# One gather of joined up and down rows per expert slot, with coefficients slot by slot on ScalarE

## The chip, the cores and the metric

The kernel runs on one core of a Trainium2 chip. The metric is the device time of one execution in microseconds (us). The engines are named as in the profile: PE (TensorE), PEld (its weight loads), DVE (VectorE), ACT (ScalarE), POOL (GpSimd) and SP (SyncE, which issues most DMAs). DMAs with indices computed on the chip are issued by POOL.

## What is computed

One layer of a streaming encoder on 512 tokens of width 2048: two groups of attention heads, then a mixer that picks experts by product keys. The change touches the expert part only. Per token, 8 heads pick 16 experts each out of 16384; an expert is one row of `u` and one row of `v`.

```python
def peer_sublayer(h, w_query, sub_keys, u, v):
    def block(hb):                                   # 128 tokens
        ...
        idx = jnp.take_along_axis(cand_i, best_j, axis=-1)        # 8 heads x 16 experts
        g = jax.nn.softmax(best_s, axis=-1)
        u_sel = jnp.take(u, idx, axis=0)
        a = jax.nn.gelu(jnp.einsum('thkd,td->thk', u_sel, hb), approximate=False)
        v_sel = jnp.take(v, idx, axis=0)
        return jnp.einsum('thk,thkd->td', (g * a).astype(hb.dtype), v_sel)
```

So per token and slot (a head's pick) there is an "up" step, the dot product of the token with a row of `u`, a Gelu and a gate, and a "down" step that adds the coefficient times a row of `v`.

## The kernel before

Attention and the projections take the first 1304 us; the change doesn't touch them. The experts are then computed in two ways side by side.

*Dense, on PE* (352 of the 512 tokens): all experts in 128 groups `j`. An **A** item multiplies the 352 tokens by the `u` of one group (48 matmuls of 352 columns, L1030), takes the Gelu on ACT and stores it to DRAM as `a_scr` (L902, L905). The last 16 products are **D** items, whose result stays on the chip. A **V** item multiplies gated activations by one half of a group's `v` (24 matmuls, L1044). Between V items, **R** items load a group's activations and gates and multiply them (`gated`: `gb` on DVE at L1049, hi part `ph` on ACT at L1051; `low`: `pl` on DVE at L1056). Every operand is split into a hi and a lo part (`split`: hi cast `wh` on ACT, L190; lo part `wl` on DVE, or for some V items on POOL, L191). Four buffers each hold a cut of weights `wh`, `wl`; an A item uses four cuts, a V item two. `cut_up` prepares the item after the one that PE works on. The gates reach the dense part by a scatter: DVE sums the gates of equal experts (`junk`, L950), and POOL writes them with 384 indirect DMAs of 128 single numbers each (L962). These are spread over the A items, four or five pieces an item. The scatters of one head wait for those of the head before.

*Sparse, by gathers* (the other 160 tokens): 160 **slots** of 128 partitions, 128 slots for the first 128 tokens ("f") and 32 for the other 32 tokens, spread over the partitions ("x"). For each slot a gather on POOL fetches 128 rows of `u` and another 128 rows of `v`, 8 KB a row, 1 MB a gather (L849). The up step is a multiply with a sum along the row on DVE (L869, followed by the read of its accumulator), the down step a multiply and add on DVE (L871). The steps go in blocks of 16: 16 up steps, then one Gelu on ACT and one multiply by the gates on DVE for all 16 slots (L874, L875), then 16 down steps. That makes 320 steps. `due` hands them out in proportion to the work of the items; a step is popped between two cuts of an A item, or after the cuts of a V item. The gather buffers are three of 8 KB a partition, and a gather is issued two steps ahead.

```python
    def consume(i):
        ...
        ahead(i + 2)
        ...
    gt = ctx.enter_context(pool("gt", 3))
```

The order on PE, DVE, ACT and SP is the order in which the code is written (`fixed`, L1081). On POOL a scheduler sets it.

Of the kernel before, what the change touches and what calls it, by code (L numbers as in the profile page):

```python
# [9 lines left out]
F32 = mybir.dt.float32  # L10
# [85 lines left out]
def hymba_peer(ctx: ExitStack, tc: tile.TileContext, xT, w_in, w_fl, b_fg, g_mix, g_q, g_k, g_merge,  # L96
               w_out, g_ffn, w_q, keysT, uT, u, v, out):
# [759 lines left out]
    def consume(i):
        if i == 0:
            ahead(0)
            ahead(1)  # L860
        ahead(i + 2)
        st, n = steps[i]
        x, s = order[st][n]
        if (st, n) == ("x", 0):
# [12 lines left out]
        yield  # L877

# [4 lines left out]
    steps = [("f", n) for n in range(2 * P)] + [("x", n) for n in range(2 * SL)]  # L883
# [3 lines left out]
    def due(n, hold=False):  # L887
# [4 lines left out]
        return [consume(i) for i in r]  # L892
# [46 lines left out]
    gt = ctx.enter_context(pool("gt", 3))  # L939
# [57 lines left out]
    def load(t):  # L997
        if t >= len(items):
# [4 lines left out]
            [(f"v{it[2]}", v[j * P:j * P + P, it[2] * H:it[2] * H + H])]  # L1003
# [143 lines left out]
def arrays_of(i):  # L1147
# [20 lines left out]
    a["u"] = c(uu.reshape(P, P, D).transpose(1, 0, 2).reshape(P * P, D))  # L1168
    a["v"] = c(np.asarray(i["peer_v"])[0].reshape(P, P, D).transpose(1, 0, 2).reshape(P * P, D))
# [20 lines left out]
```

## Time and profile before

| | us |
|---|---|
| median of 3 runs (3423.48 to 3425.88) | 3423.88 |
| the profiled execution | 3414.49 |
| its span, first to last instruction | 3412.8 |
| stretch with the scatters (1333 to 2162) | 829 |
| rest of the U products (2162 to 2394) | 232 |
| V products (2394 to the end) | 1019 |

| Engine | busy us | share |
|---|---|---|
| PE | 3259.3 | 96% |
| DVE | 2506.0 | 73% |
| POOL | 1566.5 | 46% |
| ACT | 1283.6 | 38% |

A share over the whole span is a mean over stretches with different limits, so it is read stretch by stretch. Busy time leaves out the issue of DMAs on SP and the gaps between instructions. "Idle before, releaser" is the time in which an engine stood still before an instruction, and what ended it; "issue" means that nothing in the trace ended it.

### The profile page before, as it was taken

How to read it: one execution, taken by the hardware profiler on the slowest of the kernel's cores; microseconds unless marked ns; L12 is line 12 of the kernel's file. 1: busy time of each engine (PE TensorE's matmuls, PEld its weight loads, DVE VectorE, ACT ScalarE, POOL GpSimd, SP SyncE). 2: the span in 40 equal slices, each digit the busy share in tenths (PEclk: the TensorE clock that was granted, in tenths of full speed). 3: DMA queues.
4: the chain of work that ended last, by engine and by line, in shares of the span. 5: the costliest groups of instructions: out<-in, count | busy, mean ns of one | idle time of the engine just before them, and what ended most of it. 6: DMA issues, size and time to landing. Idle time of an engine off the chain costs nothing.

```text
span 3412.8 us, 52962 instructions
## 1 busy us (share of the span) xinstructions
PE 3259.3 (96%) x19406; PEld 3057.5 (90%) x19406; DVE 2506.0 (73%) x4536; ACT 1283.6 (38%) x2452; POOL 1566.5 (46%) x1134
## 2 busy tenths in 40 slices
PE   8999999999999999988889888999999999999998
PEld 6888888888888899988888888899999999999998
DVE  7555656567547996766666666678899989899995
ACT  5544545443333333322222222334333333333332
POOL 2000000013226866787877887422444544544452
PEclk9999999999999999999999999999999999999999
DMA  3333223332443236888778777899999999998995
GB/s 121 125 102 108 91 97 104 107 103 87 144 136 112 93 127 229 293 271 275 264 263 272 268 260 269 289 339 338 375 384 363 367 368 376 353 366 348 380 362 177
DMA packets 233702, 810.85 MB, mean 238 GB/s; under 512 B 38080, under 2 KB 92480, under 8 KB 191936
## 3 DMA queue, kind: packets, MB, share of 16 engines
q1 hardware_dynamic: 169184, 448.60, 37.7%
q0 software_dynamic: 64256, 358.86, 28.2%
q8 instruction: 152, 2.49, 0.3%
q14 instruction: 110, 0.90, 0.1%
HBM read 754.41 MB, written 52.10 MB: 236 GB/s over the span
## 4 chain that ended last, share of the span: by engine, by line
PE 69%; DMA 11%; issue 8%; DVE 7%; POOL 3%; ACT 1%; SPq 0%; POOLq 0%; DVEq 0%; ACTq 0%; another core or an unknown queue 0%
PE pv L1044 21%; PE pa L1030 11%; PE pj_wo L219 5%; PE pj_wq L219 5%; DMA grf<-in_u_dram,idx 4%; DMA grf<-in_v_dram,idx 4%; PE pj_sv L219 3%; PE pj_fv L219 3%; PE pj_sk L219 3%; PE pj_fk L219 3%; PE pj_fq L219 3%; PE pj_fg L219 3%; PE pa L219 2%; PE pj_sq L219 2%; POOL g_scr L962 2%
## 5 line engine op out<-in xcount | busy, mean ns | idle before, releaser
L1044 PE MATMUL pv<-ph,wl_V 128*128 128x352 f32 x2048 | 663.0, 324 | 16.9 <-POOL wl_V L191 12.3
L1044 PE MATMUL pv<-ph,wh_V 128*128 128x352 f32 x2048 | 659.9, 322 | 0.0
L1044 PE MATMUL pv<-pl,wh_V 128*128 128x352 f32 x2048 | 659.6, 322 | 0.0
L1030 PE MATMUL pa<-dh,wl_A 128*128 128x352 f32 x1632 | 554.2, 340 | 101.8 <-DVE wl_A L191 87.3
L962 POOL DMA_INDIRECT g_scr<-tot,dst x384 | 507.1, 1321 | 133.6 <-issue 78.1
L1030 PE MATMUL pa<-dh,wh_A 128*128 128x352 f32 x1632 | 549.3, 337 | 9.7 <-ACT wh_A L190 9.0
L1030 PE MATMUL pa<-dl,wh_A 128*128 128x352 f32 x1632 | 543.2, 333 | 0.5 <-issue 0.4
L190 ACT CAST wh_V<-wr_v 128x512 fp32r<-128x512 f32 x512 | 307.8, 620 | 352.9 <-PE pv L1044 235.0
L1030 PEld LDWEIGHTS pa<-dh,wl_A 128*128 128x128 f32 x1632 | 320.5, 196 | 116.2 <-DVE wl_A L191 97.6
L190 ACT CAST wh_A<-wr_u 128x512 fp32r<-128x512 f32 x408 | 247.8, 619 | 447.7 <-PE pa L1030 353.1
L1044 PEld LDWEIGHTS pv<-ph,wl_V 128*128 128x128 f32 x2048 | 385.1, 188 | 25.1 <-POOL wl_V L191 17.6
L1044 PEld LDWEIGHTS pv<-pl,wh_V 128*128 128x128 f32 x2048 | 385.4, 188 | 0.0
L871 DVE SCALAR_TENSOR_TENSOR acc<-grf,coef,acc 128x2048 f32<-128x2048 f32 x128 | 311.3, 2432 | 100.9 <-DMA grf<-in_v_dram,idx 73.6
L1044 PEld LDWEIGHTS pv<-ph,wh_V 128*128 128x128 f32 x2048 | 385.2, 188 | 0.0
L191 DVE TENSOR_TENSOR wl_A<-wr_u,wh_A 128x512 fp32r<-128x512 f32 x404 | 276.7, 690 | 138.2 <-ACT wh_A L190 111.2
L869 DVE SCALAR_TENSOR_TENSOR grf<-grf,hbn 128x2048 f32<-128x2048 f32 x128 | 299.4, 2343 | 89.2 <-DMA grf<-in_u_dram,idx 76.3
L191 POOL TENSOR_TENSOR wl_V<-wr_v,wh_V 128x512 fp32r<-128x512 f32 x130 | 260.3, 2011 | 194.8 <-ACT wh_V L190 190.1
L191 DVE TENSOR_TENSOR wl_V<-wr_v,wh_V 128x512 fp32r<-128x512 f32 x382 | 296.4, 810 | 62.5 <-ACT wh_V L190 61.4
L1030 PEld LDWEIGHTS pa<-dh,wh_A 128*128 128x128 f32 x1632 | 322.3, 197 | 10.9 <-ACT wh_A L190 9.5
L1030 PEld LDWEIGHTS pa<-dl,wh_A 128*128 128x128 f32 x1632 | 321.0, 197 | 1.0 <-issue 1.0
L849 POOL DMA_INDIRECT grf<-in_v_dram,idx x128 | 178.8, 1397 | 217.7 <-DVE acc L871 152.7
L849 POOL DMA_INDIRECT grf<-in_u_dram,idx x128 | 172.8, 1350 | 205.2 <-DVE grf L869 123.2
(407 smaller groups left out, 6670.5 us busy)
## 6 DMA issues: line engine op xcount, KB each, us to landing
wr_u<-in_uT_dram SPq DMA_DIRECT2D x256, 512.0 KB
wr_v<-in_v_dram SPq DMA_DIRECT2D x256, 512.0 KB
g_scr<-zero POOLq DMA_DIRECT2D x16, 1408.0 KB
gg<-g_scr SPq DMA_DIRECT2D x128, 176.0 KB
a_scr<-ga SPq DMA_DIRECT2D x112, 176.0 KB
gb<-a_scr SPq DMA_DIRECT2D x112, 176.0 KB
wr_wo<-in_w_out_dram SPq DMA_DIRECT2D x32, 512.0 KB
wr_wq<-in_w_q_dram SPq DMA_DIRECT2D x32, 512.0 KB
```

The source lines that it names most:

```text
L190: nc.scalar.copy(hi, src)
L191: (lo_eng or nc.vector).tensor_tensor(lo, src, hi.bitcast(F32), op=OP.subtract)
L219: nc.tensor.matmul(ps[i][:, :hi - lo], wt[:, kk, :], ht[k][:, lo:hi], start=(k == 0 and n == 0), stop=(k == KD - 1 and n == 2))
L849: nc.gpsimd.indirect_dma_start(out=r, out_offset=None, in_=(u, v)[x], in_offset=bass.IndirectOffsetOnAxis(ap=sets[st][3][:, s:s + 1], axis=0))
L869: nc.vector.scalar_tensor_tensor(r, r, 1.0, hb, op0=OP.mult, op1=OP.mult, accum_out=dt[:, s:s + 1])
L871: nc.vector.scalar_tensor_tensor(ac, r, cf[:, s:s + 1], ac, op0=OP.mult, op1=OP.add)
L962: w = nc.gpsimd.indirect_dma_start(out=g_flat, out_offset=bass.IndirectOffsetOnAxis(ap=dst[:, b, s:s + 1], axis=0), in_=tot[:, b, s:s + 1] ...
L1030: nc.tensor.matmul(ps[:, :TD], wt[:, k % 4, :], ht[k], start=(k == 0 and n == 0), stop=(k == KD - 1 and n == 2))
L1044: nc.tensor.matmul(po["now"][n][:, :TD], w_, a, start=(jj == 0 and pi == 0), stop=(jj == JC - 1 and pi == 2))
```

## The change

The rows of `u` and `v` of an expert stand side by side in one DRAM table `uv` (16384 rows of 16 KB). One gather per slot fetches both, 2 MB a gather. There are two buffers of 16 KB a partition in place of three of 8 KB, and a gather is issued one slot ahead. A slot's work is a generator with two pieces: up step, Gelu and multiply by the gate (both on ACT, 128 x 1 each); then the down step. `due` puts both pieces behind one another into an item's work. The blocks of 16 and DVE's multiply of 16 coefficients are gone. The dense part reads its `v` out of the right half of `uv`.

```diff
-    def orders(n):
-        return [(x, b * TOPK + i) for b in range(n // TOPK) for x in range(2) for i in range(TOPK)]
-
-    order = {"f": orders(P), "x": orders(SL)}
     rows = {}
     sets = {"f": (hbn, acc, g0, idx0, dots, coef)}

-    def fetch(st, n):
-        if n < len(order[st]):
-            x, s = order[st][n]
-            r = rows[st, n] = gt.tile([P, D], F32, name=f"gr{st}{x}_{s}", tag="gr")
+    def ahead(i):
+        for st, s in steps[i:i + 1]:
+            r = rows[i] = gt.tile([P, 2 * D], F32, name=f"gr{st}_{s}", tag="gr")
             nc.gpsimd.indirect_dma_start(
-                out=r, out_offset=None, in_=(u, v)[x],
+                out=r, out_offset=None, in_=uv,
                 in_offset=bass.IndirectOffsetOnAxis(ap=sets[st][3][:, s:s + 1], axis=0))
...
     def consume(i):
         if i == 0:
             ahead(0)
-            ahead(1)
-        ahead(i + 2)
...
+        ahead(i + 1)
...
-        r = rows.pop((st, n))
-        if x == 0:
-            nc.vector.scalar_tensor_tensor(r, r, 1.0, hb, op0=OP.mult, op1=OP.mult, accum_out=dt[:, s:s + 1])
-        else:
-            nc.vector.scalar_tensor_tensor(ac, r, cf[:, s:s + 1], ac, op0=OP.mult, op1=OP.add)
-        if x == 0 and s % TOPK == TOPK - 1:
-            c = slice(s - TOPK + 1, s + 1)
-            nc.scalar.activation(cf[:, c], dt[:, c], AF.Gelu)
-            nc.vector.tensor_tensor(cf[:, c], cf[:, c], g[:, c], op=OP.mult)
-        return
+        r = rows.pop(i)
+        c = slice(s, s + 1)
+        nc.vector.scalar_tensor_tensor(r[:, :D], r[:, :D], 1.0, hb, op0=OP.mult, op1=OP.mult,
+                                       accum_out=dt[:, c])
+        nc.scalar.activation(cf[:, c], dt[:, c], AF.Gelu)
+        nc.scalar.activation(cf[:, c], cf[:, c], AF.Copy, scale=g[:, c])
         yield
+        nc.vector.scalar_tensor_tensor(ac, r[:, D:], cf[:, c], ac, op0=OP.mult, op1=OP.add)
...
-    steps = [("f", n) for n in range(2 * P)] + [("x", n) for n in range(2 * SL)]
+    steps = [("f", n) for n in range(P)] + [("x", n) for n in range(SL)]
...
-        return [consume(i) for i in r]
+        return [x for i in r for x in (consume(i),) * 2]
...
-    gt = ctx.enter_context(pool("gt", 3))
+    gt = ctx.enter_context(pool("gt", 2))
...
-            [(f"v{it[2]}", v[j * P:j * P + P, it[2] * H:it[2] * H + H])]
+            [(f"v{it[2]}", uv[j * P:j * P + P, D + it[2] * H:D + it[2] * H + H])]
```

On POOL, among the scatters of the A items, the order before was this. `g_scr` rows are scatters, `grf` rows gathers. In brackets stand the semaphores that a row waits for: DMASW0 to DMASW7 are those of POOL's own earlier DMAs, used in turn.

```order
L849 DMA grf_9_14460<-in_u_dram,idx_8879 128x2048 [waits DMASW7_49,DVE_49]
L962 DMA g_scr<-tot,dst 5771264x1 [waits DMASW0_49,DVE_49]
L962 DMA g_scr<-tot,dst 5771264x1 [waits DMASW1_49,DVE_49]
L962 DMA g_scr<-tot,dst 5771264x1 [waits DMASW2_49,DVE_49]
L962 DMA g_scr<-tot,dst 5771264x1 [waits DMASW3_49,DVE_49]
L962 DMA g_scr<-tot,dst 5771264x1 [waits DMASW4_49,DVE_49]
L849 DMA grf_10_14463<-in_u_dram,idx_8879 128x2048 [waits DMASW5_49,DVE_49]
L849 DMA grf_11_14546<-in_u_dram,idx_8879 128x2048 [waits DMASW6_49,DVE_49]
L962 DMA g_scr<-tot,dst 5771264x1 [waits DMASW7_49,DVE_49]
```

About the same place with the change:

```order
L844 DMA grf_14541<-in_uv_dram,idx_8879 128x4096 [waits DMASW0_49,DVE_49]
L948 DMA g_scr<-tot,dst 5771264x1 [waits DMASW1_49,DVE_49]
L948 DMA g_scr<-tot,dst 5771264x1 [waits DMASW2_49,DVE_49]
L948 DMA g_scr<-tot,dst 5771264x1 [waits DMASW3_49,DVE_49]
L948 DMA g_scr<-tot,dst 5771264x1 [waits DMASW4_49,DVE_49]
L844 DMA grf_14709<-in_uv_dram,idx_8879 128x4096 [waits DMASW5_49,DVE_49]
L948 DMA g_scr<-tot,dst 5771264x1 [waits DMASW6_49,DVE_49]
L948 DMA g_scr<-tot,dst 5771264x1 [waits DMASW7_49,DVE_49]
L948 DMA g_scr<-tot,dst 5771264x1 [waits DMASW0_49,DVE_49]
```

A gather has twice the columns, and four or nine scatters stand between two gathers, where it was none to six. A gather stands on POOL behind the scatters whose sums come before the up step of the slot two before it, since its buffer is free when that slot's down step is done. Each DMA waits for the semaphore of the one eight places before it, in both.

On DVE, among the V items, the order before was this (`wl_V` rows are lo parts of weights for PE, `gb` and `pl` the multiply and the low part of an R item, `acc` rows down steps):

```order
L871 SCALAR_TENSOR_TENSOR acc<-grf_86_25744,coef,acc 128x2048
L191 TENSOR_TENSOR wl_V_31_25897<-wr_v_31_25814,wh_V_31_25896 128x512
L191 TENSOR_TENSOR wl_V_31_25901<-wr_v_31_25814,wh_V_31_25900 128x512
L1049 TENSOR_TENSOR gb_25810<-gb_25810,gg_25812 128x352
L871 SCALAR_TENSOR_TENSOR acc<-grf_87_25783,coef,acc 128x2048
L1056 TENSOR_TENSOR pl_25910<-gb_25810,ph_25905 128x352
L191 TENSOR_TENSOR wl_V_16_25939<-wr_v_16_25853,wh_V_16_25938 128x512
```

A like place among the V items with the change (`grf` is an up step):

```order
L191 TENSOR_TENSOR wl_V_5_24797<-wr_v_5_24717,wh_V_5_24796 128x512
L191 TENSOR_TENSOR wl_V_5_24801<-wr_v_5_24717,wh_V_5_24800 128x512
L1035 TENSOR_TENSOR gb_24713<-gb_24713,gg_24715 128x352
L858 SCALAR_TENSOR_TENSOR grf_24683,dots<-grf_24683,hbn 128x2048
L863 SCALAR_TENSOR_TENSOR acc<-grf_24683,coef,acc 128x2048
L1042 TENSOR_TENSOR pl_24817<-gb_24713,ph_24809 128x352
L191 TENSOR_TENSOR wl_V_7_24884<-wr_v_7_24794,wh_V_7_24883 128x512
```

Between two pairs of lo parts stood one step; now the up and the down step of a slot stand there together, and the items next to them have none.

## Rows read from the trace of the kernel before

**Rows 1.** The page: busy us (share) of PE; slices of PE and POOL.

```profile
PE 3259.3 (96%) x19406; PEld 3057.5 (90%) x19406; DVE 2506.0 (73%) x4536; ACT 1283.6 (38%) x2452; POOL 1566.5 (46%) x1134
...
PE   8999999999999999988889888999999999999998
...
POOL 2000000013226866787877887422444544544452
```

**Rows 2.** Busy us by stretch (instructions): PE, PEld, DVE, ACT, POOL, clock, DMA.

```profile
1333.00:2162.00 829.00, 723.83 (x4133) 709.45 (x4133) 558.71 (x1289) 242.57 (x434) 661.52 (x496) 0.94 0.79 270
2162.00:2394.00 232.00, 227.52 (x1376) 225.60 (x1375) 173.14 (x200) 85.71 (x159) 54.91 (x40) 0.99 0.90 330
2394.00:3413.00 1019.00, 994.34 (x6193) 985.53 (x6191) 898.97 (x997) 357.84 (x636) 482.30 (x298) 1.00 0.92 351
```

**Rows 3.** Groups by line, POOL, 1333 to 2162: busy, mean ns, idle before.

```profile
L962 POOL DMA_INDIRECT g_scr<-tot,dst x384 | 507.1, 1321 | 133.6 <-issue 78.1 <-DVE junk L950 28.8 <-DMA g_scr<-tot,dst 17.3
L849 POOL DMA_INDIRECT grf<-in_u_dram,idx x61 | 84.8, 1390 | 26.5 <-DVE junk L950 12.5 <-issue 12.2 <-DMA grf<-in_u_dram,idx 0.9
L849 POOL DMA_INDIRECT grf<-in_v_dram,idx x51 | 71.6, 1404 | 15.5 <-issue 11.9 <-DVE junk L950 3.0 <-DVE wl_A L191 0.3
```

**Rows 4.** Timeline from 1803 us: start, duration, what [idle before <-releaser].

```profile
1803.01 0.97 POOL L962 DMA_INDIRECT g_scr<-tot,dst  x1 [0.30 <-issue]
1803.77 2.29 DVE L869 SCALAR_TENSOR_TENSOR grf<-grf,hbn 128x2048 f32<-128x2048 f32 x1 [2.58 <-DMA grf<-in_u_dram,idx]
1804.28 2.62 POOL L962 DMA_INDIRECT g_scr<-tot,dst  x1 [0.31 <-issue]
```

**Rows 5.** Groups by line, DVE, 1333 to 2162: up and down steps.

```profile
L869 DVE SCALAR_TENSOR_TENSOR grf<-grf,hbn 128x2048 f32<-128x2048 f32 x63 | 144.0, 2290 | 82.3 <-DMA grf<-in_u_dram,idx 69.4 <-issue 12.8
L871 DVE SCALAR_TENSOR_TENSOR acc<-grf,coef,acc 128x2048 f32<-128x2048 f32 x49 | 115.1, 2350 | 90.2 <-DMA grf<-in_v_dram,idx 63.3 <-issue 26.8
```

**Rows 6.** Timeline, 1659 to 1668 us: a gather and the step for it.

```profile
1659.87 0.98 POOL L849 DMA_INDIRECT grf<-in_u_dram,idx  x1 [0.30 <-issue]
...
1667.72 2.29 DVE L869 SCALAR_TENSOR_TENSOR grf<-grf,hbn 128x2048 f32<-128x2048 f32 x1 [8.38 <-DMA grf<-in_u_dram,idx]
```

**Rows 7.** Timeline, 2590 to 2601 us: two gathers, a lo part, a step.

```profile
2590.77 1.24 POOL L849 DMA_INDIRECT grf<-in_v_dram,idx  x1
...
2592.31 0.94 POOL L849 DMA_INDIRECT grf<-in_v_dram,idx  x1 [0.30 <-DVE gb L1049]
...
2599.66 1.29 POOL L191 TENSOR_TENSOR wl_V<-wr_v,wh_V 128x512 fp32r<-128x512 f32 x1 [1.40 <-ACT wh_V L190]
2600.34 2.76 DVE L871 SCALAR_TENSOR_TENSOR acc<-grf,coef,acc 128x2048 f32<-128x2048 f32 x1 [1.85 <-DMA grf<-in_v_dram,idx]
```

**Rows 8.** Groups by line, ACT, 1333 to 2162: hi casts, Gelu of the products.

```profile
L190 ACT CAST wh_A<-wr_u 128x512 fp32r<-128x512 f32 x344 | 209.4, 619 | 401.0 <-PE pa L1030 312.5 <-issue 39.1 <-DVE junk L950 16.6
L902 ACT ACTIVATE ga<-pa 128x352 f32<-128x352 f32 x86 | 39.9, 464 | 163.7 <-DMA a_scr<-ga 115.3 <-issue 33.3 <-PE pa L1030 14.9
```

**Rows 9.** Timeline, 2893 to 2897 us: from an up step to its coefficients.

```profile
2893.02 0.69 DVE L191 TENSOR_TENSOR wl_V<-wr_v,wh_V 128x512 fp32r<-128x512 f32 x1
...
2896.27 0.09 DVE L869 DVE_READ_ACCUMULATOR grf<-grf,hbn 128x1 f32 x1
2896.39 0.22 ACT L874 ACTIVATE coef<-dots 128x16 f32<-128x16 f32 x1 [1.73 <-DVE grf L869]
...
2896.64 0.20 DVE L875 TENSOR_TENSOR coef<-coef,g 128x16 f32<-128x16 f32 x1 [0.28 <-ACT coef L874]
```

**Rows 10.** Groups by line, 2394 us to the end: PE, DVE and POOL.

```profile
L1044 PE MATMUL pv<-ph,wl_V 128*128 128x352 f32 x2048 | 663.0, 324 | 16.9 <-POOL wl_V L191 12.3 <-DVE wl_V L191 4.1
...
L191 DVE TENSOR_TENSOR wl_V<-wr_v,wh_V 128x512 fp32r<-128x512 f32 x380 | 295.1, 811 | 61.5 <-ACT wh_V L190 60.4 <-issue 0.5
L191 POOL TENSOR_TENSOR wl_V<-wr_v,wh_V 128x512 fp32r<-128x512 f32 x130 | 260.3, 2011 | 194.8 <-ACT wh_V L190 190.1 <-issue 2.5 <-PE pv L1044 1.4
...
L1049 DVE TENSOR_TENSOR gb<-gb,gg 128x352 f32<-128x352 f32 x112 | 58.1, 518 | 0.0
```

More of the change, by code (lines that the diff above doesn't have):

```diff
@@ L96, in hymba_peer @@
 def hymba_peer(ctx: ExitStack, tc: tile.TileContext, xT, w_in, w_fl, b_fg, g_mix, g_q, g_k, g_merge,
-               w_out, g_ffn, w_q, keysT, uT, u, v, out):
+               w_out, g_ffn, w_q, keysT, uT, uv, out):
     nc = tc.nc
@@ L834, in hymba_peer @@
     bigx.close()
-    def orders(n):
-        return [(x, b * TOPK + i) for b in range(n // TOPK) for x in range(2) for i in range(TOPK)]
-    order = {"f": orders(P), "x": orders(SL)}
     rows = {}
     sets = {"f": (hbn, acc, g0, idx0, dots, coef)}
-    def fetch(st, n):
-        if n < len(order[st]):
-            x, s = order[st][n]
-            r = rows[st, n] = gt.tile([P, D], F32, name=f"gr{st}{x}_{s}", tag="gr")
+    def ahead(i):
+        for st, s in steps[i:i + 1]:
+            r = rows[i] = gt.tile([P, 2 * D], F32, name=f"gr{st}_{s}", tag="gr")
             nc.gpsimd.indirect_dma_start(
-                out=r, out_offset=None, in_=(u, v)[x],
+                out=r, out_offset=None, in_=uv,
                 in_offset=bass.IndirectOffsetOnAxis(ap=sets[st][3][:, s:s + 1], axis=0))
-    def ahead(i):
-        for st, n in steps[i:i + 1]:
-            fetch(st, n)
     def consume(i):
@@ L859, in consume @@
             ahead(0)
-            ahead(1)
-        ahead(i + 2)
-        st, n = steps[i]
-        x, s = order[st][n]
-        if (st, n) == ("x", 0):
+        ahead(i + 1)
+        st, s = steps[i]
+        if (st, s) == ("x", 0):
             start_x()
         hb, ac, g, _, dt, cf = sets[st]
-        r = rows.pop((st, n))
-        if x == 0:
-            nc.vector.scalar_tensor_tensor(r, r, 1.0, hb, op0=OP.mult, op1=OP.mult, accum_out=dt[:, s:s + 1])
-        else:
-            nc.vector.scalar_tensor_tensor(ac, r, cf[:, s:s + 1], ac, op0=OP.mult, op1=OP.add)
-        if x == 0 and s % TOPK == TOPK - 1:
-            c = slice(s - TOPK + 1, s + 1)
-            nc.scalar.activation(cf[:, c], dt[:, c], AF.Gelu)
-            nc.vector.tensor_tensor(cf[:, c], cf[:, c], g[:, c], op=OP.mult)
-        return
+        r = rows.pop(i)
[4 more added lines that the diff above has]
+        nc.scalar.activation(cf[:, c], cf[:, c], AF.Copy, scale=g[:, c])
         yield
+        nc.vector.scalar_tensor_tensor(ac, r[:, D:], cf[:, c], ac, op0=OP.mult, op1=OP.add)
     def start_x():
@@ L1167, in arrays_of @@
     a["uT"] = c(uu.reshape(P, P, KD, P).transpose(1, 3, 2, 0))
-    a["u"] = c(uu.reshape(P, P, D).transpose(1, 0, 2).reshape(P * P, D))
-    a["v"] = c(np.asarray(i["peer_v"])[0].reshape(P, P, D).transpose(1, 0, 2).reshape(P * P, D))
+    vv = np.asarray(i["peer_v"])[0]
+    a["uv"] = c(np.concatenate([x.reshape(P, P, D).transpose(1, 0, 2).reshape(P * P, D) for x in (uu, vv)], axis=1))
     return a
```

## The prediction

> **What bounds the kernel now.** I read the busy table and the slices first [rows 1]. PE is busy 96% of the span, but its line drops to 8 in slices 18 to 25 (with one 9 between them), and just there POOL's line is at 7 and 8. The table by stretches says the same in us [rows 2]. The program runs three kinds of work after 1333 us:
>
> - 1333 to 2162 us, "scatter phase": A items (U products) with 384 scatters and 112 gathers on POOL. PE runs 4133 matmuls, or 86.1 items of 48, in 829 us: 9.63 us an item, at a mean granted clock of 0.94 of the upper level (2.4 GHz).
> - 2162 to 2394, "tail": the same products, no scatter. 1376 matmuls, 28.7 items, 8.09 us an item, clock 0.99.
> - 2394 to 3413, "V phase": PE busy 994 of 1019 us, DVE 899, clock 1.00.
>
> So the scatter phase loses about 86.1 x (9.63 - 8.09) = 132 us to something that is not PE. It is POOL. Its busy time is 661.5 us [rows 2], and before each DMA there is a dead 0.30 us that the trace calls "issue", also when nothing is waited for [rows 4]; 496 x 0.30 = 149 us. Together that is 810 of 829 us, and only some 20 us are real waits (17.3 of them scatters that wait for an earlier DMA [rows 3]). DVE's waits for gathers (69 and 63 us [rows 5]) and PE's stalls behind DVE are then consequences: POOL issues its DMAs late, and everything in program order behind them is late too.
>
> In the V phase POOL is no bound. PE's own stalls there are 16.9 us, mostly behind the lo parts that POOL computes [rows 10].
>
> **What the change removes.** One gather per slot in place of two: in the scatter phase 56 POOL instructions fewer. An undisturbed one costs 0.97 + 0.30 = 1.27 us [rows 4]; the means are 1.39 to 1.40 [rows 3], so with the gap 1.70. The difference is time in which POOL stands still behind a DVE step: a scatter that starts at 1804.28, with a DVE step running from 1803.77 to 1806.06, takes 2.62 us [rows 4]. There are as many long DVE steps afterwards (one up and one down per slot, as now), so I take this stand-still as kept and price the gather at 1.27: 56 x 1.27 = **-71 us**. Ends: -95 (56 x 1.70) if the stand-still goes with the gather; 0 if a gather of rows twice as long costs twice as much. I choose near the first, since a scatter of 4-byte rows and a gather of 8 KB rows both take 0.97 to 0.98 [rows 4, 6]: the size isn't in it.
>
> The Trainium skill has a rule on this (SBUF — State Buffer, "Who interferes with whom"): a VectorE instruction with two SBUF inputs and a GpSimd instruction that reads SBUF exclude each other for a whole instruction. By that rule the stand-still belongs to DVE's steps and the lower price is right; a view that counts POOL's means would give the higher one. The 2.62 us of [rows 4] agree with the rule.
>
> The 10 small multiplies of coefficients on DVE go too, 0.20 us each [rows 9]: 2 us, hidden.
>
> **What it adds.** (a) *Landing.* A gather of 1 MB that DVE waits for takes 7.85 us from its start on POOL (1659.87 to 1667.72 [rows 6]). For 2 MB the nearest rows are two 1 MB gathers back to back in the V phase: the second is there 9.57 us after the first started (2590.77 to 2600.34 [rows 7]). The other end is twice one, 15.7. I take 9.6 to 11, because two such gathers are the same bytes on the same queue. It matters in two places. The order shows that a POOL DMA waits for the one eight before it; eight DMAs at 829/496 = 1.67 us are 13.4 us, more than 11, so that wait costs nothing. And a gather now stands on POOL right behind the release of its buffer by the down step two slots before, so it has the spacing of two slots (three items carry two: 3 x 8.09 = 24 us) less the 5.2 us of the slot between to land. Then the first scatter of each head waits for the last of the head before; seven such places cost 17.3 us now [rows 3], and a scatter behind a 2 MB gather lands 1.7 us (9.57 - 7.85) or more later: 7 x 1.7 = **+12** (0 to +35).
>
> (b) *ScalarE in the chain.* Within a slot, up, Gelu, multiply and down now follow each other. From the end of the read of the accumulator (2896.36) to a DVE instruction behind one ScalarE instruction are 0.28 us, 0.22 of them the Gelu [rows 9]; with a second of the same size 0.50 us. In the scatter phase this lies under POOL's time. ScalarE is also held there until up is done, where before this was so once in 16 slots; the cuts behind it wait on DVE in any case.
>
> (c) *DVE held in one piece.* A slot takes 2.29 + 0.09 + 0.50 + 2.35 = 5.23 us between two cuts of weights [rows 5, 9], where one step took 2.35. With a gate row's multiply (0.52 [rows 10]) and its low part, which I take to be as long, 6.27. What PE allows: four buffers of cut weights, each used for 1019/512 = 1.99 us in the V phase, so 7.96, less the hi cast of 0.62 [rows 8] and two lo parts of 0.69 [rows 9]: 5.96 us. So a slot with a gate row is 0.3 late, one without is not. Of the 320 steps 112 lie in the scatter phase [rows 5] and 39 in the tail (its 40 POOL instructions but one [rows 2]); that leaves 169 for the V phase, 84.5 slots: half of them x 0.3 = 13 us. DVE has 120 us idle there [rows 2] and needs 84.5 x 0.5 = 42 of them for the new gaps. Some of the lateness will carry over to the next item, so I take twice the 13: **+25** (0 to +101, below). In the tail a cut lasts 8.09/4 = 2.02 us and few slots carry a gate row: 20 slots, **+3** (0 to half a us each, +10).
>
> **Sum.** -71 + 12 + 25 + 3 = -31 us. The profiled execution took 3414.5 us (span 3412.8), so 3383 there; the median of the runs is 3423.9, 9.4 us above it, and I carry the difference over: **3393 us**, 0.9% less. Its own range, from the neighbouring values of each term, is 3370 to 3412.
>
> **Rivals.**
>
> *More is saved (0.10).* The whole 1.70 per gather, and DVE's waits on landings (133 us [rows 5]) shorten because one landing of 9.6 replaces two of 7.85. The floor is PE's pace of the tail, -132 us; I take -95 and +10 for the V phase: 3339. For it: POOL and DVE wait on the same thing in this phase. Against: POOL's own issue time bounds, not landings. The Trainium skill's fit (DMA: Bandwidth & Descriptors, "Anatomy of one DMA — SWDGE (gpsimd) path") of 2.0 us plus bytes over 436 GB/s would give 6.8 us for 2 MB as an estimate, against 4.4 twice, which speaks for this rival; its 4.4 is well under the 7.85 that the trace has for 1 MB.
>
> *Another chain takes over (0.16).* ScalarE already waits 115 us in the scatter phase for stores of ga to land [rows 8]. When POOL gives time back, the loop store, next Gelu, cut, load may hold at some 9.3 us an item: 86.1 x (9.63 - 9.3) = 28 saved, less 28 of cost: 3424, no change.
>
> *DVE becomes the bound of the V phase (0.14).* Every slot starts late by the 0.50 gap and by one blocked POOL lo part (mean 2.01, free 1.29 [rows 7, 10]: 0.7): 84.5 x 1.2 = 101 us on PE. -71 + 12 + 3 + 101 = +45: 3469, slower. It decides from 56/84.5 = 0.66 us a slot. For: DVE is 88% busy there. Against: idle 120 us, 60.4 of them waits for hi casts that wait for PE, so DVE is ahead [rows 2, 10].
>
> *The long gather stops POOL (0.10).* If it lands after 15.7 us, POOL meets the wait for the eighth DMA before: about one gather in eight DMAs, so a cycle of 15.7 in place of 829/56 = 14.8 now: +50, no saving; with 12, 25 and 3 it is 3514. It decides from 14.8. That a gather of 16 KB rows costs POOL double (0 saved, 3464) is in the same chance.
>
> **Chances.** Forecast 0.50. A measurement of this kernel tells about 0.2% (7 us) from no change. Faster: 0.48 of the forecast, 0.10, and 0.03 of the second rival = 0.61. Same: 0.02 + 0.10 = 0.12. Slower: 0.03 + 0.14 + 0.10 = 0.27. Range: 3340 leaves out half of the first rival, 3460 most of the last two: 3340 to 3460.
>
> **What would show it.** Right: the phase with scatters shrinks from 829 to about 770 us, POOL there still near 100% with its 0.30 gaps, gathers on POOL at 1.0 to 1.4 us, 56 of them; gather landings of 9.6 to 11; the V phase 1019 to about 1044 with more PE stalls behind lo parts. Wrong: POOL with waits on DMAs or on DVE's down step of over 50 us in the scatter phase (another bound), gathers of over 2 us in the mean (price by bytes), a V phase over 1075 us or one not longer at all.

## The result, and the profile after

The changed kernel takes 3510.9 us in the median (3489.9 to 3512.5, four runs), the kernel before 3423.7 beside it: 2.4% slower, ratio 1.0241 (95% interval 1.0202 to 1.0280). Forecast were 3393 us and a range of 3340 to 3460. The profiled execution has a span of 3510.8 us, 98.0 more than before (before, the profiled execution lies 9 us under the median).

The page of the changed kernel, busy time and POOL's slices:

```profile
PE 3302.8 (94%) x19406; PEld 3071.0 (87%) x19406; DVE 2502.4 (71%) x4526; ACT 1325.9 (38%) x2762; POOL 1372.4 (39%) x974
...
POOL 2000000012238765778876654001334333333342
```

POOL has lost 194 us of work [rows 1], and its line falls from 8 to 6, 5 and 4 towards the end of the scatter phase. By stretch (scatter phase, tail, V phase; columns: length, busy of PE, PEld, DVE, ACT, POOL with instructions, clock, DMA share, GB/s):

```profile
1323.97:2158.55 834.58, 737.11 (x4134) 709.20 (x4133) 563.09 (x1277) 252.02 (x541) 594.53 (x439) 0.94 0.74 271
2158.55:2429.65 271.10, 243.76 (x1410) 237.19 (x1408) 175.97 (x205) 92.29 (x200) 22.76 (x20) 0.96 0.76 284
2429.65:3510.80 1081.15, 1012.55 (x6193) 992.59 (x6192) 891.70 (x998) 385.71 (x801) 388.95 (x214) 0.99 0.87 332
```

Measured from the first scatter to the last, the scatter phase of before is 827.8 us long, its tail 232.2, its V phase 1018.9 [rows 2, nearly]. So it is +7, +39 and +62, less 10 us because the first scatter comes earlier: +98. The 71 us that POOL was to give back are not there, and two stretches in which POOL is no bound got longer. Not all of that is waiting: PE's own busy time is 16 us longer in the tail, with 34 matmuls more and at a granted clock of 0.96 against 0.99, and 18 us longer in the V phase, at 0.99 against 1.00 [rows 2]; no run takes this share apart.

POOL's groups in the scatter phase (busy, mean ns, idle before and what ended it), then its waits there (us, times, longest):

```profile
L948 POOL DMA_INDIRECT g_scr<-tot,dst x383 | 517.2, 1350 | 154.7 <-issue 81.1 <-DMA g_scr<-tot,dst 32.1 <-DVE junk L936 27.0
L844 POOL DMA_INDIRECT grf<-in_uv_dram,idx x56 | 77.4, 1381 | 86.7 <-DVE acc L863 73.3 <-issue 7.3 <-DVE junk L936 4.9
```

```profile
POOL g_scr L948 <- issue: 81.1, 246, 1.8
POOL grf L844 <- DVE acc L863: 73.3, 14, 13.9
POOL g_scr L948 <- DMA g_scr<-tot,dst: 32.1, 17, 3.5
POOL g_scr L948 <- DVE junk L936: 27.0, 84, 1.0
```

The gathers wait 73.3 us for a down step (`acc`), where [rows 3] has no such wait. The scatters' 32.1 us for landings (17.3 before) come from another place than before. Twelve of them are longer than 1 us, and in eleven, 28 us together, the DMA eight places before the waiting scatter is a gather that started 12.1 to 13.7 us earlier. One of them, with seven scatters between the two rows:

```profile
1982.66 1.16 POOL L844 DMA_INDIRECT grf<-in_uv_dram,idx  x1 [0.31 <-issue]
...
1995.88 1.36 POOL L948 DMA_INDIRECT g_scr<-tot,dst  x1 [2.96 <-DMA g_scr<-tot,dst]
```

The profile names a scatter there, one of those issued right behind the gather; the place, eleven times the same, points to the gather's landing. In the trace of before, the five waits over 1 us stand at other distances from a gather, all near the change from one head to the next.

ACT in the same stretch (groups by line: busy, mean ns, idle before and what ended it), then DVE:

```profile
L190 ACT CAST wh_A<-wr_u 128x512 fp32r<-128x512 f32 x342 | 199.2, 614 | 131.9 <-PE pa L1016 116.1 <-DVE junk L936 9.2 <-remote 3.0
L888 ACT ACTIVATE ga<-pa 128x352 f32<-128x352 f32 x86 | 39.7, 462 | 235.7 <-DMA a_scr<-ga 151.4 <-PE pa L1016 43.1 <-issue 30.4
...
L860 ACT ACTIVATE coef<-dots 128x1 f32<-128x1 f32 x56 | 11.4, 203 | 213.1 <-DVE grf L858 210.1 <-issue 3.0
```

```profile
L191 DVE TENSOR_TENSOR wl_A<-wr_u,wh_A 128x512 fp32r<-128x512 f32 x343 | 236.8, 691 | 228.8 <-ACT wh_A L190 152.8 <-ACT ga L888 38.9 <-issue 23.8
L863 DVE SCALAR_TENSOR_TENSOR acc<-grf,coef,acc 128x2048 f32<-128x2048 f32 x56 | 131.7, 2351 | 33.5 <-ACT coef L861 29.3 <-ACT coef L860 4.2
L858 DVE SCALAR_TENSOR_TENSOR grf<-grf,hbn 128x2048 f32<-128x2048 f32 x56 | 127.9, 2284 | 4.7 <-issue 4.7
```

ACT stands 210 us behind up steps. Its hi casts waited 312.5 us for PE [rows 8], which is the sign of an engine that is ahead; now they wait 116.1. DVE waits for hi casts 152.8 us, and no longer for landings (133 us in [rows 5], here none). In the trace of before, the waits of ACT for up steps and of DVE for hi casts were these in the scatter phase:

```profile
ACT coef L874 <- DVE grf L869: 18.2, 2, 12.1
DVE wl_A L191 <- ACT wh_A L190: 67.2, 41, 5.4
```

One place shows how it hangs together; timeline of ACT, DVE and POOL (start, duration, idle before and what ended it):

```profile
2025.14 0.46 ACT L888 ACTIVATE ga<-pa 128x352 f32<-128x352 f32 x1 [4.43 <-DMA a_scr<-ga]
...
2025.51 0.61 ACT L190 CAST wh_A<-wr_u 128x512 fp32r<-128x512 f32 x1
2026.15 0.69 DVE L191 TENSOR_TENSOR wl_A<-wr_u,wh_A 128x512 fp32r<-128x512 f32 x1 [4.46 <-issue]
2026.76 2.28 DVE L858 SCALAR_TENSOR_TENSOR grf<-grf,hbn 128x2048 f32<-128x2048 f32 x1
...
2029.08 0.20 ACT L860 ACTIVATE coef<-dots 128x1 f32<-128x1 f32 x1 [2.97 <-DVE grf L858]
2029.32 0.29 ACT L861 ACTIVATE coef<-coef,g 128x1 f32<-128x1 f32 x1
2029.52 1.64 ACT L190 CAST wh_A<-wr_u 128x512 fp32r<-128x512 f32 x3
2029.65 2.35 DVE L863 SCALAR_TENSOR_TENSOR acc<-grf,coef,acc 128x2048 f32<-128x2048 f32 x1 [0.60 <-ACT coef L861]
...
2032.27 1.18 POOL L844 DMA_INDIRECT grf<-in_uv_dram,idx  x1 [6.11 <-DVE acc L863]
```

ACT waits 4.43 us for a store of `ga`, then casts one cut. DVE takes its lo part and the up step. ACT, next in order at the coefficient, waits 2.97 us for the up step, and three casts stand behind it. The down step follows, and only when it is done can POOL start the next gather, for which it has stood 6.11 us with scatters behind it. The Trainium skill calls the queues of ScalarE, VectorE and GpSimd "strict FIFO" (PSUM — Partial Sum Buffer, "Engine vs sequencer instructions"); this trace agrees: the three casts start at 2029.52, right behind the coefficient's two instructions, and none of them ahead.

The V phase, waits of ACT and of PE, then ACT's wait for PE in the trace of before:

```profile
ACT coef L860 <- DVE grf L858: 112.5, 53, 3.1
ACT wh_V L190 <- PE pv L1030: 108.1, 109, 2.6
ACT coef L860 <- DVE grx L858: 67.5, 32, 3.5
...
PE pv L1030 <- POOL wl_V L191: 30.4, 30, 1.8
PE pv L1030 <- DVE wl_V L191: 14.8, 13, 3.0
PE pv L1030 <- DVE accd L1048: 13.9, 8, 2.0
```

```profile
ACT wh_V L190 <- PE pv L1044: 235.0, 217, 1.8
```

ACT stands 180 us behind up steps there too (14 before), its lead over PE is halved (108.1 us of waits for PE, 235.0 before), and PE stalls 59 us where it was 16.9 [rows 10].

### The profile page after: what moved, and what is told of

Same layout as the page of the kernel before. It is cut to its first block, busy times and chain, and to the rows that moved or that the text cites. A ratio compares the mean times of both kernels' runs of the same rounds, so it can differ in the third digit from the quotient of the medians.

```text
span 3510.8 us, 52646 instructions
## 1 busy us (share of the span) xinstructions
PE 3302.8 (94%) x19406; PEld 3071.0 (87%) x19406; DVE 2502.4 (71%) x4526; ACT 1325.9 (38%) x2762; POOL 1372.4 (39%) x974
## 3 DMA queue, kind: packets, MB, share of 16 engines
q0 software_dynamic: 41216, 358.85, 26.0%
## 4 chain that ended last, share of the span: by engine, by line
PE 63%; DVE 13%; issue 10%; DMA 8%; ACT 3%; POOL 3%; SPq 0%; another core or an unknown queue 0%; DVEq 0%; POOLq 0%; ACTq 0%
PE pv L1030 15%; PE pa L1016 12%; DMA a_scr<-ga 5%; PE pj_wo L219 5%; PE pj_wq L219 5%; DVE grf L858 4%; PE pj_sv L219 3%; PE pj_fv L219 3%; PE pj_sk L219 3%; PE pj_fk L219 3%; POOL wl_V L191 3%; PE pj_fq L219 3%; PE pj_fg L219 3%; PE pa L219 2%; PE pj_sq L219 2%
## 5 line engine op out<-in xcount | busy, mean ns | idle before, releaser
L1016 PE MATMUL pa<-dh,wh_A 128*128 128x352 f32 x1632 | 556.4, 341 | 44.4 <-ACT wh_A L190 42.7
L948 POOL DMA_INDIRECT g_scr<-tot,dst x384 | 518.1, 1349 | 155.0 <-issue 81.4
L191 POOL TENSOR_TENSOR wl_V<-wr_v,wh_V 128x512 fp32r<-128x512 f32 x130 | 291.4, 2260 | 370.1 <-ACT wh_V L190 272.5
L844 POOL DMA_INDIRECT grf<-in_uv_dram,idx x128 | 162.2, 1267 | 528.1 <-DVE acc L863 498.7
L190 ACT CAST wh_V<-wr_v 128x512 fp32r<-128x512 f32 x512 | 298.2, 616 | 167.8 <-PE pv L1030 108.1
L191 DVE TENSOR_TENSOR wl_V<-wr_v,wh_V 128x512 fp32r<-128x512 f32 x382 | 304.4, 832 | 76.8 <-ACT wh_V L190 76.6
L190 ACT CAST wh_A<-wr_u 128x512 fp32r<-128x512 f32 x408 | 238.2, 614 | 160.4 <-PE pa L1016 138.5
L355 POOL TENSOR_TENSOR osq<-o 128x512 f32<-128x512 f32 x14 | 14.5, 1037 | 527.0 <-ACT o L349 527.0
```

The source lines that it names most:

```text
L190: nc.scalar.copy(hi, src)
L191: (lo_eng or nc.vector).tensor_tensor(lo, src, hi.bitcast(F32), op=OP.subtract)
L355: nc.gpsimd.tensor_tensor(sq, r, r, op=OP.mult)
L844: nc.gpsimd.indirect_dma_start(out=r, out_offset=None, in_=uv, in_offset=bass.IndirectOffsetOnAxis(ap=sets[st][3][:, s:s + 1], axis=0))
L948: w = nc.gpsimd.indirect_dma_start(out=g_flat, out_offset=bass.IndirectOffsetOnAxis(ap=dst[:, b, s:s + 1], axis=0), in_=tot[:, b, s:s + 1] ...
L1016: nc.tensor.matmul(ps[:, :TD], wt[:, k % 4, :], ht[k], start=(k == 0 and n == 0), stop=(k == KD - 1 and n == 2))
```

## The experiments

Three theories. **H**: DVE is held in one piece by up and down back to back. **S**: ScalarE, in order, stands behind each up step, so the hi casts behind it are late. **G**: the gather of 16 KB rows (or the dense `v` with rows 16 KB apart) costs the time. The stretches of all kernels, each measured in its profiled execution from the first scatter, the last scatter and the first V product (us):

| kernel | median | ratio to before (95%) | scatter phase | tail | V phase |
|---|---|---|---|---|---|
| before | 3423.7 | 1 | 828 | 232 | 1019 |
| after | 3510.9 | 1.0241 (1.0202-1.0280) | 835 | 271 | 1081 |
| e1_spread | 3459.1 | 1.0115 (1.0092-1.0138) | 786 | 249 | 1089 |
| e2_spread_late | 3412.5 | 0.9968 (0.9958-0.9979) | 782 | 247 | 1048 |
| e3_no_coef | 3462.1 | 1.0111 (1.0085-1.0136) | 827 | 265 | 1048 |
| e4_two_gathers | 3522.1 | 1.0289 (1.0266-1.0312) | 857 | 258 | 1082 |
| e5_coef_ahead | 3456.6 | 1.0087 (1.0064-1.0110) | 798 | 252 | 1077 |
| e7_v_apart | 3406.8 | 0.9945 (0.9926-0.9965) | 779 | 249 | 1043 |
| e8_ga3 | 3383.8 | 0.9877 (0.9855-0.9900) | 782 | 230 | 1047 |
| e9_two_late | 3445.0 | 1.0074 (1.0055-1.0093) | 829 | 241 | 1038 |
| e10_before_ga3 | 3422.7 | 0.9982 (0.9969-0.9996) | 838 | 229 | 1026 |
| e11_after_ga3 | 3473.1 | 1.0141 (1.0112-1.0170) | 810 | 252 | 1083 |
| e12_coef_gated | 3394.7 | 0.9900 (0.9866-0.9934) | 787 | 250 | 1024 |
| e13_gated_ga3 | 3364.7 | 0.9825 (0.9796-0.9854) | 769 | 234 | 1024 |

The kernel before was timed again beside each group of kernels, with medians of 3422.5 to 3427.3, so the ratios are what to compare. The line between scatter phase and tail is the last scatter, and PE does not always stand at the same product there: it ran 4090 to 4212 matmuls of U products in the scatter phase. So up to some 20 us can pass from one of the two stretches to the other; their sum is free of this.

**e1_spread: the two pieces of a slot apart.**

```diff
+    halves = [x for i in range(len(steps)) for x in (consume(i),) * 2]
-    nwork = len(steps)
+    nwork = len(halves)
...
-        return [x for i in r for x in (consume(i),) * 2]
+        return [halves[i] for i in r]
```

> The changed kernel, with the two pieces of a slot handed out one at a time, as the 320 steps were before: `due` counts pieces and not slots, so that about two lo parts or some scatters stand on DVE between a slot's up and its down. The coefficient stays on ScalarE right behind the up step. Theory H (DVE held in one piece of 5.2 us makes every engine late): the V phase falls from 1081 to about 1020-1030 us, the tail from 271 to 235, ScalarE's wait for the up step in the scatter phase halves, and the time is 3350-3420. Theory S (ScalarE stands in order behind each up step, so the hi casts behind it are late): the coefficient still stands right behind each up, ScalarE still waits about 200 us for up steps in the scatter phase, and the time is 3470-3510. Theory G (the 16 KB gather or the row stride of the dense v): 3500-3515.

3459 us, between the theories. The scatter phase falls by 48 us and the tail by 22 (the first V product comes 64 us earlier), the way that H has it, though the tail stays over its 235, and ScalarE's wait for up steps in the scatter phase, which H halves, grows from 210 to 252 us. POOL's wait for down steps is nearly gone (scatter phase):

```profile
POOL grf L844 <- DVE acc L863: 10.6, 4, 3.7
```

But the V phase, for which H gave 1020 to 1030, stays at 1089, and ScalarE waits even longer there, as S has it:

```profile
ACT coef L860 <- DVE grf L858: 147.6, 51, 7.2
ACT coef L860 <- DVE grx L858: 101.5, 32, 6.3
...
PE pv L1031 <- POOL wl_V L191: 51.8, 31, 2.4
```

So H fits the times before the V phase, and S the V phase. In the scatter phase ScalarE's lead is no measure of the loss: its hi casts wait only 78 us for PE here, less than the 116 of the changed kernel, and the stretch is shorter.

**e2_spread_late: besides, the coefficient ahead of the down step.**

```diff
-        nc.scalar.activation(cf[:, c], dt[:, c], AF.Gelu)
-        nc.scalar.activation(cf[:, c], cf[:, c], AF.Copy, scale=g[:, c])
         yield
+        nc.scalar.activation(cf[:, c], dt[:, c], AF.Gelu)
+        nc.scalar.activation(cf[:, c], cf[:, c], AF.Copy, scale=g[:, c])
```

> As e1_spread, and Gelu and multiply moved from behind the up step to right ahead of the down step, so that on ScalarE the hi casts of the cuts between them stand ahead of the coefficient. DVE then waits for two short ScalarE instructions ahead of each down. Theory S: here the loss goes, ScalarE's wait for up steps falls under 50 us in the scatter phase, time 3340-3400, at least 50 us under e1_spread. Theory H: same as e1_spread within 15 us. Theory G: 3500-3515.

3412.5 us, 47 under e1_spread by the medians (50 by the ratios) and now 0.3% faster than before: the direction and nearly the size that S gives, though over its 3340 to 3400. 41 us of it are the V phase; ScalarE's waits for up steps fall from 249 to 36 us there. What it still has over before in the V phase, 29 us, stands beside two waits of DVE, for landings (57 us, 20 before) and for coefficients (46 us):

```profile
DVE grf L858 <- DMA grf<-in_uv_dram,idx: 31.6, 15, 4.0
...
DVE acc L863 <- ACT coef L862: 27.4, 28, 1.0
DVE grx L858 <- DMA grx<-in_uv_dram,idx: 25.1, 9, 4.4
DVE ac L863 <- ACT coef L862: 18.5, 20, 1.0
```

**e3_no_coef: no instruction on ScalarE in the slot.**

```diff
-        nc.scalar.activation(cf[:, c], dt[:, c], AF.Gelu)
-        nc.scalar.activation(cf[:, c], cf[:, c], AF.Copy, scale=g[:, c])
...
-        nc.vector.scalar_tensor_tensor(ac, r[:, D:], cf[:, c], ac, ...)
+        nc.vector.scalar_tensor_tensor(ac, r[:, D:], g[:, c], ac, ...)
```

> The changed kernel without the Gelu and the multiply on ScalarE; the down step takes the gate itself as its coefficient. It leaves out the Gelu of the sparse tokens and makes their up step useless. Up and down stay back to back on DVE, without the 0.60 us gap between. Theory S: ScalarE never waits for an up step, the hi casts run ahead again, time 3340-3420. Theory H: DVE is still held 4.65 us in one piece, time 3460-3500 (84 gaps of 0.6 us less in the V phase, 50 us at most). Theory G: 3500-3515.

3462 us. The V phase gives back 33 of its 62 us, the scatter phase only 8: there POOL's wait for down steps is even longer, without any coefficient:

```profile
POOL grf L844 <- DVE acc L861: 125.8, 36, 13.3
```

So ScalarE's part in the slot is not what holds the scatter phase. Most of what can be had there comes by taking up and down apart (e1_spread). In this kernel the gap of 0.60 us between up and down is gone too, so the 33 us of the V phase belong to ScalarE's waits and to that gap together.

**e4_two_gathers: the joining alone undone.**

```diff
-            nc.gpsimd.indirect_dma_start(
-                out=r, out_offset=None, in_=uv, ...
+            for x, tab in enumerate((u, v)):
+                nc.gpsimd.indirect_dma_start(
+                    out=r[:, x * D:x * D + D], out_offset=None, in_=tab, ...
```

> The changed kernel with two tables again: two gathers of 8 KB rows into the two halves of the slot's 16 KB buffer, and the dense v read from its own table. Order of the pieces, coefficients and buffers as in the changed kernel. So it undoes the joining alone. Theory G (the long gather or the strided v costs the time): back to 3420-3450. Theories S and H: POOL has 56 gathers more in the scatter phase again; if POOL is no longer the bound there, the time stays at 3505-3530, if it is, up to 3580 (56 x 1.27 = 71).

3522 us, not faster than the changed kernel: with two gathers of 8 KB rows, in two tables (the dense `v` reads its own again), the loss is as large, so G is not the main cause. The run gives POOL its 56 instructions back as well, so it cannot show that the long gather costs nothing: scatters wait 11.7 us for landings here, 32.1 in the changed kernel. With the joining, the scatter phase is 22 us shorter and the tail 13 longer; e4_two_gathers has 78 matmuls more in its scatter phase, so the sum, 10 us, is the better figure.

**e9_two_late: the same undoing in the mended order of e2_spread_late** (the diff against e2_spread_late is that of e4_two_gathers).

> As e2_spread_late, with two tables again: two gathers of 8 KB rows into the halves of the slot's buffer (the dense v from its own table). So against e2_spread_late it shows what the joining of gathers is worth once the order is mended. If POOL bounds the scatter phase in this order, 56 gathers more cost 40 to 71 us there: scatter phase 822-850, time 3450-3485. If POOL is no longer the bound, as with e4_two_gathers against the changed kernel (11 us): 3410-3430.

3445 us, 33 more than e2_spread_late by the medians, 36 by the ratios; the scatter phase is where the first branch has it (822 to 850), the time 5 us under it. The scatter phases of e2_spread_late and of this:

```profile
1333.79:2115.47 781.68, 709.97 (x4106) 694.04 (x4106) 552.68 (x1273) 258.82 (x541) 610.36 (x439) 0.96 0.79 284
```

```profile
1331.87:2161.15 829.28, 727.90 (x4139) 715.25 (x4140) 558.26 (x1278) 262.78 (x545) 669.22 (x496) 0.93 0.77 270
```

57 POOL instructions fewer take 47.6 us off the scatter phase (33 matmuls, about 6 us, pass into the tail): here the joining does what it was forecast to do, at two thirds of the size. In tail and V phase the joined kernel is 15 us longer.

**e7_v_apart: dense `v` from a table of its own, in e2_spread_late.**

```diff
-            [(f"v{it[2]}", uv[j * P:j * P + P, D + it[2] * H:D + it[2] * H + H])]
+            [(f"v{it[2]}", v[j * P:j * P + P, it[2] * H:it[2] * H + H])]
```

> As e2_spread_late, with the dense v read out of a table of its own (rows 8 KB apart) and not out of the right half of the joined table (rows 16 KB apart). The gathers stay joined. Theory G': the row stride slows the dense loads, V phase 1048 to about 1020, time 3380-3390. Otherwise no change: 3405-3417.

0.9945 against 0.9968, with intervals that overlap; V phase 1043 against 1048. If the stride of the rows costs anything, it is a few us, not the 20 to 29.

**e5_coef_ahead: the coefficient earlier, ahead of the cuts of the item of the down step.** `coefficient(i)` puts the Gelu and the multiply of slot `i` on ScalarE, once.

```diff
+        for i in r:
+            if i % 2:
+                coefficient(i // 2)
         return [halves[i] for i in r]
```

> As e2_spread_late, but Gelu and multiply stand on ScalarE ahead of all cuts of the item in which the down step falls (not right ahead of the down step). They then wait only for an up step of an item before. In e2_spread_late DVE waited 46 us for coefficients in the V phase and 7 in the scatter phase. If those waits are what keeps its V phase at 1048 us (1019 in the kernel before), the V phase falls to 1019-1030 and the time to 3380-3395. If what is left there is something else (landings of the 16 KB gathers, for which DVE waited 57 us there), nothing moves: 3405-3417. If ScalarE gets held by the earlier place (an up step that stands late on DVE), it is slower, 3420-3440.

3457 us, by the ratios some 41 slower than e2_spread_late: the third branch, and more of it than the 3420 to 3440 expected. V phase 1077, with ScalarE behind up steps again:

```profile
ACT coef L853 <- DVE grf L866: 95.4, 37, 5.1
ACT coef L853 <- DVE grx L866: 66.0, 23, 5.5
```

**e12_coef_gated: among the V items, the coefficient behind the hi casts of an item and ahead of `ph`.**

```diff
+            if kind(t) == "V":
+                for i in list(coefs):
+                    coefficient(i)
             if prev[0] == "R":
                 g, ph = gated(prev[1])
```

> As e2_spread_late, but among the V items Gelu and multiply stand on ScalarE right behind the hi casts of an item and ahead of the cast ph of its R item, on which DVE's gate multiply has to be done first. In e2_spread_late DVE waits 46 us for coefficients in the V phase; a wait for ph that waits for DVE stands ahead of them. If this order is it, DVE's wait for coefficients falls under 15 us, and the V phase from 1048 to 1025-1040: 3385-3405. If up steps stand late on DVE there, ScalarE is held by them again as in e5_coef_ahead (1077) and it gets slower: 3420-3440.

3395 us, V phase 1024, only 5 over before. ScalarE waits 63 us for up steps, and DVE's waits for coefficients are down from 46 us to under 2. The four places of the same two short instructions (behind the up step, ahead of the casts, right ahead of the down step, behind the casts) give V phases of 1089, 1077, 1048 and 1024 us.

**e8_ga3, e10_before_ga3, e11_after_ga3: a third buffer of `ga`**, in e2_spread_late, in the kernel before and in the changed kernel.

```diff
-        g = dn.tile([P, TD], F32, name=f"ga{j}", tag="ga")
+        g = dn.tile([P, TD], F32, name=f"ga{j}", tag="ga", bufs=3)
```

> As e2_spread_late, with three buffers of ga (Gelu of the dense products, waiting for its store to DRAM) in place of two. ScalarE waited 171 us for these stores in the scatter phase of e2_spread_late, 111 in the kernel before. If the loop of store, next Gelu, cut and lo part is what eats the rest of the 71 us that fewer gathers should give (46 seen), the scatter phase falls from 782 to about 755 us and the time to 3380-3390. If ScalarE waits there because it is early (it has nothing else to do), the wait moves to PE's products and the time stays: 3403-3417.

3384 us, some 30 less, but not where it was expected: the scatter phase stays at 782, the tail falls from 247 to 230 (the profiled executions differ by 21 in all, so some 9 us are not placed). So the time lies in the first branch, but not for its reason. ScalarE's 171 us behind stores are gone in the scatter phase, and its hi casts wait 311 us for PE in place of 190: it was early there. POOL gains nothing: its scatters take 21 us longer and wait 14 us longer for landings, its gathers take 20 us less.

> The kernel before, with three buffers of ga in place of two and nothing else. If the store loop of ga is a limit of its own that was there all along, the kernel before gains about as much as e2_spread_late did from it (29 us): 3390-3400. If POOL's DMAs set the pace of its scatter phase and the loop only holds a kernel whose POOL has time left, it gains under 10 us, and what it gains lies in the tail: 3414-3424.

3422.7 us, under 0.2% less, the second branch: the kernel before does not need it.

> The changed kernel, with three buffers of ga in place of two and nothing else. ScalarE waits 151 us for these stores there in the scatter phase, 44 in the tail. If the loss of the changed kernel came from the store loop taking over as the bound (a rival of the prediction), most of the 87 us go: 3430-3450. If it comes from ScalarE and DVE being held by up and down steps, 10 to 30 us go at most, mainly in the tail (271 us): 3480-3500.

3473 us, 34 less by the ratios and 38 by the medians: more than expected and far from all; 25 in the scatter phase, 19 in the tail (66 matmuls, about 11 us, pass from the tail into the scatter phase), nothing in the V phase. POOL's wait for down steps falls with it, but its scatters, 1350 ns in the mean of the changed kernel, get longer:

```profile
POOL grf L844 <- DVE acc L863: 9.5, 2, 7.1
```

```profile
L948 POOL DMA_INDIRECT g_scr<-tot,dst x384 | 565.8, 1473 | 157.8 <-issue 84.9 <-DVE junk L936 37.9 <-DMA g_scr<-tot,dst 26.6
```

So in the changed kernel the store loop is one link of the chain seen at 2025 us: ScalarE waits for a store, DVE's slot comes late, POOL stands behind the slot. Without that wait POOL's gathers come through, and of the 64 us of waits that go, 49 come back as longer scatters: every scatter over 1.5 us long overlaps an up or down step, as in the trace of before. So a wait that is gone is not yet time won. The phase is at 810 against 782 to 786 in the spread orders; that the slot in one piece makes this difference fits, but no run has the third buffer and e1_spread's edit alone. The Trainium skill says that the same gap repeating on the engine that should be saturated can mean that there are too few buffers for the next tile (Perfetto Trace Analysis, "Optimization Strategy"). ScalarE, 38% busy, is not that engine in either kernel, and the runs go both ways: the third buffer gives 34 to 38 us here, and next to nothing in the kernel before, where the gap is 115 us [rows 8].

**e13_gated_ga3: e12_coef_gated with the third buffer.**

> e12_coef_gated with three buffers of ga: all that helped, if both help. The two lie in different stretches (V phase; scatter phase and tail), so they should add: e8_ga3 (3384) less what e12_coef_gated gains over e2_spread_late (3412): 3360-3380. If e12_coef_gated gains nothing: 3380-3392.

3364.7 us, ratio 0.9825 (0.9796 to 0.9854) to before, within the 3360 to 3380 expected: in the time the two gains add. Its stretches:

```profile
1334.35:2103.65 769.30, 701.76 (x4121) 695.18 (x4122) 554.63 (x1273) 265.32 (x539) 612.13 (x439) 0.95 0.81 288
2103.65:2337.31 233.66, 228.54 (x1388) 227.07 (x1386) 175.93 (x205) 92.70 (x195) 31.37 (x20) 0.99 0.87 331
2337.31:3361.30 1023.99, 998.07 (x6193) 987.83 (x6192) 884.54 (x998) 396.16 (x801) 371.65 (x214) 0.99 0.92 350
```

The scatter phase is 58 us shorter than before, tail and V phase are back within about 5 us. The gains were to lie in different stretches, yet 12 us and more of the scatter phase (769 against 782 and 787) are in neither kernel alone; why is open. This is the joined gather with its pieces, its coefficients and `ga` in places that suit it.

## Why the prediction was wrong, point by point

Two steps failed. The text let the hi casts "wait on DVE in any case", so it gave ScalarE's new waits for up steps no price; they are most of what the V phase lost beyond the forecast. And it gave no price to POOL's gathers waiting in order for a down step (73.3 us) and took the wait for the eighth DMA before as nothing (28 us); these took back all that fewer gathers saved.

**The gathers on POOL (-71): the price was right, what came next was not.** POOL's gathers fall from 156.4 us [rows 3] to 77.4, the gaps by 57 x 0.30 = 17. Scatters grow by 10 (517.2 us against 507.1). Together POOL does 84 us less (busy -67, gaps -17). Beside that stand 73.3 us of waits for down steps and 15 more of scatters for landings: 88, so nothing is left. The text had named this among its signs of failure ("waits on DMAs or on DVE's down step of over 50 us"), but gave it no price and no chance. The joining does bring 48 us where its surroundings let it (e9_two_late to e2_spread_late). POOL saves 72 us of gathers and 17 of gaps there; its scatters take 12 us longer (1367 ns in the mean against 1331), and it waits 33 us more for the sums (`junk`). The stand-still was kept, as the prediction assumed: in the scatter phases of before, of the changed kernel and of e2_spread_late every POOL DMA over 1.5 us overlaps an up or down step, and what those DMAs take over 0.97 us is 142, 131 and 146 us in all.

**Landing: near in size, wrong in its effect.** DVE waited for no landing in the scatter phase of the changed kernel. Where it waited elsewhere, from the gather's start to the up step for it:

```profile
2840.61 1.23 POOL L844 DMA_INDIRECT grf<-in_uv_dram,idx  x1
...
2852.27 2.79 DVE L858 SCALAR_TENSOR_TENSOR grf<-grf,hbn 128x2048 f32<-128x2048 f32 x1 [0.70 <-DMA grf<-in_uv_dram,idx]
```

That is 11.66 us in the V phase (five such, 11.4 to 11.9). In the scatter phase of e2_spread_late twelve such waits end 9.9 to 12.8 us after the start, where 9.6 to 11 was forecast. The text held the wait for the eighth DMA before for free, since eight DMAs take 13.4 us in the mean and the long gather stops POOL from 14.8 us on. But a mean was the wrong measure: between two DVE steps scatters follow each other every 1.27 us, eight of them are through in some 10 us, and POOL then stands until the gather has landed. That is the 28 us of scatter waits above; with two 8 KB gathers (e4_two_gathers) all waits of scatters for landings come to 11.7 us. For DVE the landing matters only in the spread order: in the V phase of e2_spread_late a gather starts 14.2 us in the median ahead of its up step, with landings of up to 14.3, hence DVE's 57 us of waits; in the changed kernel it is 18.2. The Trainium skill's fit gave 6.8 us as an estimate (DMA: Bandwidth & Descriptors, "Anatomy of one DMA — SWDGE (gpsimd) path"); the measurement, 11.4 to 11.9 us, decides.

**Head boundaries (+12): right in size by luck.** Scatters wait 32.1 us for landings, 17.3 before: +15. But 28 of them are the eighth-DMA wait; of the waits over 1 us only one, of 2.20 us, is left near a change of heads, where before there were five.

**ScalarE in the chain: the step that failed first.** The text says that ScalarE is held until up is done, but "the cuts behind it wait on DVE in any case". They don't. Each cut goes ScalarE, then DVE, and in the kernel before ScalarE ran ahead, up to the four buffers of cuts. With a wait for DVE in ScalarE's order at every slot, the lead goes: its waits for PE fall from 312.5 to 116.1 us in the scatter phase and from 235.0 to 108.1 in the V phase. e2_spread_late and e12_coef_gated give 41 and 65 us of the V phase back against e1_spread by this place alone. In the scatter phase the lost lead is not the loss: e3_no_coef has 252 us of such waits again and a scatter phase of 827, e1_spread 78 us and 786.

**DVE held in one piece (+25 in the V phase, +3 in the tail, 0 in the scatter phase): mis-sized, and in the wrong stretch.** The gap between up and down was 0.60 us, not 0.50. In the V phase about 29 us remain without any ScalarE instruction (e3_no_coef, 1048), which is near the +25; the other 33 of the 62 are ScalarE's and the gap's. In the scatter phase, where the piece got no price and only its gap was put "under POOL's time", taking it apart brings 48 us (e1_spread): a gather waits on POOL, in order, for the down step. The tail lost 39 us, and 3 were forecast: 22 come back by spreading, 17 more by the third `ga` buffer in the spread order.

**The rivals.** "Another chain takes over", the store loop, named a real link: 34 to 38 us of the loss (e11_after_ga3), but as part of a loss, not as the floor of a gain. "DVE becomes the bound" put +101 on the V phase, where 62 were lost, about as far off as the forecast's +25; e1_spread, where DVE hardly waits for a coefficient any more, still has 1089, and e12_coef_gated, with the same steps on DVE and the same instructions on ScalarE, 1024; so a DVE that is held 1.2 us longer in each slot is not the mechanism. "The long gather stops POOL" named 3514, and 3510.9 was measured: luck, since its condition (a landing of over 14.8 us) was not met and its price by bytes neither (gathers of 1381 ns in the mean); what is true of it is the 28 us. The range ended at 3460 because each rival stood for one stretch; the losses of three stretches came together.

What stays open: how the changed kernel's scatter phase splits exactly between the slot in one piece, the store loop and the landing eight DMAs before, since the first two alone bring 48 and 25 us and together (e8_ga3, with the later coefficient) no more than the spreading, and the third has no run of its own.

## What to carry to other kernels

An instruction that is put on another engine is priced by what it waits for there and by what stands behind it in that engine's order, not by its own 0.2 us: the same two ScalarE instructions cost the V phase 65 us more or less by their place. An engine that is idle because it is ahead (its waits end on the bound engine) may hold slack that others live on, as in the V phase here; a change that lets it wait for a slower neighbour spends it. It may also hold none, as in the scatter phase: an experiment tells. When a bound engine gets time back, list the waits that its instructions carry in the new order before counting the saving, and hand long pieces out singly. A wait for an instruction a fixed number of places before is priced by the fastest run of instructions between the two, not by their mean pace.

## What was not expected of the hardware

A gather of 16 KB rows takes POOL 0.98 us undisturbed, the same as one of 8 KB rows [rows 6], and the transfers of that queue need 41216 packets in place of 64256 for the same 359 MB. No higher rate goes with it: the core moves 332 GB/s in the V phase of the changed kernel and 342 to 350 in the better ones, 351 before. On ScalarE a Gelu of 128x1 takes 0.20 us, where 128x16 took 0.22 [rows 9], and the multiply by a column 0.29 to 0.30: one slot at a time costs nearly as much each as sixteen together.
